# Strassen weight sums: from help in spare buffers to an adding transfer inside the raw buffer

## The chip, the cores and the metric

The kernel runs on one core of one Trainium2 chip. The metric is the device time of one execution in microseconds, as the median of the runs. A core has the engines TensorE (PE, with its weight loads shown apart as PEld), VectorE (DVE), ScalarE (ACT), GpSimd (POOL) and SyncE (SP), each of which works through its own queue in order, and 16 DMA engines that move data after SP, POOL or ACT has issued a transfer.

## The reference

One decoder block on x of 256 tokens by 4096 channels, all in float32:

```
h    = rmsnorm(x, norm_w)
proj = h @ w_in                     # 4096 x 20480: u_p z_p u_c b_c c_c z_c (2048 each), g_logit (8192)
y_pool = (pooled(u_p) @ pool_w) * pool_scale * silu(z_p)      # windows 2, 4, 8, 16, one per group of 512
y_conv = b_c * conv3(c_c * u_c) * silu(z_c)                   # causal, depthwise
br     = y_pool @ w_branch[0], y_conv @ w_branch[1]           # 2048 x 4096 each
merged = sum over both of sigmoid(g_logit + gate_b) * br
out    = rmsnorm(x + merged @ w_out, final_norm_w)            # 4096 x 4096
```

Nearly all of the arithmetic is in the products with `w_in`, `w_branch` and `w_out`: 256 rows against weights that are each used once.

## The kernel before

**Units and steps.** A unit produces 1024 output columns for all 256 tokens: `cu0`, `cc0`, `cz0`, `cb0` (the convolution branch), the same with 1, `pz`/`pu` (pooling), eight gate units `g0_0` to `g1_3`, eight branch units `b0_0` to `b1_3`, and four output units `o0` to `o3`. A unit of the input projection has 16 steps; each consumes one raw weight block of 256 x 1024, loaded as 128 partitions x 2048 floats (1024 KB) into one of `NRAW` raw buffers.

**Precision.** A float32 product is made of three fast ones: each operand is split into a high part (ACT copies it to the type fp32r) and a low part (DVE subtracts the high part from the original), and PE computes high x high, high x low, low x high. The split weights lie in a ring of `RING` KB per partition (class `Ring`, lines 211 to 238), from which a block is taken in preparation and returned as PE finishes with it.

**P and S steps.** A P step multiplies the block directly: 24 matmuls of 128 x 512. An S step uses a variant of Strassen's scheme on the 2 x 2 quarters q0, q1, q2, q3 of the block (128 x 512 each) and needs 21 matmuls, with seven weight operands: q1, q2, q3 as they are, and four sums. Before, these are V = (q0 + q1, q0 + q2), then W0 = V0 + q2 and W1 = W0 + q3. The other operands of the products, sums of quarters of the activations, are made once for each activation block (`sums_s`, lines 902 to 908). Of the 448 blocks of P and S steps, 216 belong to S steps. Which places in a unit are S steps is in the table `PLACES`.

**What an S step's preparation is** (`Step.micros`, lines 291 to 325): DVE makes V (`sums`), ACT copies q1 to q3 (`direct`), DVE makes W0, the low parts of q1 to q3 and W1, then ACT and DVE split V (`t13`) and W (`t24`). In some steps, the helped ones, V isn't made by DVE: q0 is loaded twice into a half of a finished result tile (E or R) while that stands empty, and a POOL transfer adds q1 and q2 to it on its way from HBM (`place_of_sum`, and lines 1269 to 1287 of `pump`). The table `HELPED` lists the candidates, and a candidate whose place isn't free in time isn't helped. 60 S steps are helped, 156 are not.

**What sets the order.** `tc.keep_in_program_order` fixes every engine's order to the order in which the program emits. `pump` (line 1257), called after each group of matmuls, emits loads (when the raw buffer that they go to has been released), adds, and the preparation of coming steps, up to `AHEAD` = 3 steps ahead of the step that PE multiplies and as far as the ring has room. Between these, `tick` emits one item of a queue of other work every six matmuls: joins of finished sums, activations, transposes, stores, fills. SP issues the weight loads, POOL the other transfers.

**The opening.** In the first unit, `cu0`, x is still being loaded. Steps 2 to 9 each also square a part of x for the first norm (`square`, line 1094): ACT squares 1024 columns (the first straight into `sq`, the others into V), and DVE adds V to `sq`. At step 10 PE sums `sq` over partitions, DVE makes the reciprocal root and two diagonal matrices, and at step 11 PE multiplies these out (`spread`, line 1114).

Of the kernel before, what the change touches and what calls it, by code (L numbers as in the profile page):

```python
# [26 lines left out]
F32 = mybir.dt.float32  # L27
# [18 lines left out]
RING = 62  # L46
NRAW = 3
# [9 lines left out]
def hybrid_block(ctx: ExitStack, tc: tile.TileContext, x, x_t, norm_t, w_first, w_in, pool_w, pool_scale,  # L57
# [8 lines left out]
    pin = tc.keep_in_program_order  # L66

# [21 lines left out]
    def move(dst, src):  # L89

        return pin(nc.gpsimd.dma_start(dst, src))
# [18 lines left out]
    V = sb("V", [P, 2, NH])  # L110
    W = sb("W", [P, 2, NH])
# [60 lines left out]
    warm = V[:, 0, 0:P].bitcast(BF16)  # L172
# [74 lines left out]
    def place_of_sum(i):  # L247

        return (E, R)[i // 2][:, i % 2].rearrange("p (i n) -> p i n", i=2)


    class Step:
# [7 lines left out]
        def micros(self):  # L260
# [30 lines left out]
            if self.kind == "S":  # L291
                q = r.rearrange("p (i n) -> p i n", i=4)

                helped = self.slot is not None
                v = place_of_sum(self.slot) if helped else V
# [22 lines left out]
                def t24(block):  # L318
                    self.b24 = block
                    t = piece(block, 0, 8).rearrange("p (i a n) -> p i a n", i=2, a=2)  # L320
                    self.h24, self.l24 = t[:, :, 0], t[:, :, 1]
                    act(self.h24, W)
                    sub(self.l24, W, self.h24.bitcast(F32))

                return self.pre + self.post + ([] if helped else [(0, None, sums)]) + [(12, lambda: not helped or self.added, direct), (8, None, t13), (8, None, t24)]
# [31 lines left out]
        def groups(self):  # L357
# [27 lines left out]
            elif self.kind == "S":  # L385
# [3 lines left out]
                         "N5": (Q5, self.h13, self.l13, 0, ("F", 0, 1)),  # L389
                         "N7": (Q7, self.h13, self.l13, 1, ("F", 1, 0)),  # L390
                         "N6": (Q6, self.h24, self.l24, 0, ("F", 1, 1)),
                         "N4": (A22, self.h24, self.l24, 1, ("E", 1, 1))}
                order = ("N3", "M2", "N4", "M1", "N5", "N7", "N6") if self.closing else (
                    "M1", "N3", "M2", "N5", "N7", "N6", "N4")
                v = self.op.block
                left = {}
                for nm in order:
                    o, h, l, i, bank = prods[nm]
                    mm = [(v(0, o), h[:, i]), (v(0, o), l[:, i]), (v(1, o), h[:, i])]
                    block = {"M": self.bd, "N": self.bd}[nm[0]] if nm in ("M1", "N3", "M2") else (  # L400
                        self.b13 if nm in ("N5", "N7") else self.b24)
# [77 lines left out]
    sums_from = [None, None]  # L479

    def e_done(n=2, which=0):

        def f():
            sums_from[which] = now[0] + n
        return f
# [57 lines left out]
    def put(dst, src):  # L543

        for k in range(2):
            move(dst[:, :, 1 - k], src.rearrange("p (q k) t -> p q k t", k=2)[:, :, k])
# [1090 lines left out]
```

## Time and profile before

| | |
|---|---|
| median of 3 runs | 2359.65 us (2359.35 to 2360.26) |
| profiled execution, first to last instruction (the span) | 2357.9 us |
| profiled execution's own time, span and what lies around it | no figure apart from the span is recorded; the median of the runs is 1.75 us above the span |
| PE, DVE, ACT, POOL busy | 2344.5, 2204.8, 1426.4, 125.0 us |
| moved by DMA | 597.89 MB, 254 GB/s on average |
| mean granted TensorE clock | 0.998 |

Rows of the profile read as follows. A row of the timeline has the start in us from the span's start, the length in us, the engine, the line of the kernel, the operation, what is written and read by the tiles' names, the size and how many instructions were merged (x2: two in a row); in brackets stands the idle time before it and what ended that. A row of waits says who waited for whom: us in total, times, the longest. Lines 69 and 72 are the helpers by which ACT's and DVE's operations are recorded, so operations are told apart by tiles and sizes: `ring<-raw` of 128x1536 on DVE are the low parts of q1 to q3 of an S step, `W<-W,raw` its second W.

### The profile page before, as it was taken

The numbers are of one execution on the slowest core, as the hardware profiler recorded it, in microseconds if no ns is written. First come the engines' busy times: TensorE is split into PE (matmuls) and PEld (weight loads), VectorE is DVE, ScalarE is ACT, GpSimd is POOL, SyncE is SP. The second block draws the span as 40 slices with busy tenths as digits, with TensorE's granted clock in tenths as the row PEclk, the third lists the DMA queues.
The fourth block names the chain that finished last, engine by engine and source line by source line (L and its number), as shares of the span: only waits on it lengthen the run. The fifth ranks groups of instructions, "written<-read, shape, count | busy, mean of one in ns | idle before, by whom it ended". The sixth has DMA issues, their size and how long they took to land.

```text
span 2357.9 us, 28175 instructions
## 1 busy us (share of the span) xinstructions
PE 2344.5 (99%) x10456; PEld 1941.8 (82%) x10456; DVE 2204.8 (94%) x2278; ACT 1426.4 (60%) x1485; POOL 125.0 (5%) x180
## 2 busy tenths in 40 slices
PE   9999999999999999999999999999999999999998
PEld 7888888888888888888888888888888888888886
DVE  8999999989999989989999999999999899898998
ACT  7555665656556556566565656665665556566564
POOL 0000000000002002000000000000000000000000
PEclk9999999999999999999999999999999999999999
DMA  8567787866877758757887887898866668777777
GB/s 336 182 229 228 238 272 256 272 231 215 269 262 250 234 218 258 230 220 248 263 267 259 286 270 243 259 302 289 292 237 233 246 244 306 225 244 274 253 235 269
DMA packets 110347, 597.89 MB, mean 254 GB/s; under 512 B 11504, under 2 KB 11760, under 8 KB 56704
## 3 DMA queue, kind: packets, MB, share of 16 engines
q1 hardware_dynamic: 89584, 508.37, 59.5%
q0 software_dynamic: 20192, 86.65, 15.7%
q8 instruction: 82, 1.34, 0.2%
q10 hardware_dynamic: 432, 1.07, 0.1%
q14 instruction: 57, 0.47, 0.1%
HBM read 563.20 MB, written 25.49 MB: 250 GB/s over the span
## 4 chain that ended last, share of the span: by engine, by line
PE 99%; DMA 0%; DVE 0%; ACT 0%; SPq 0%; DVEq 0%; issue 0%
PE sums L1336 72%; PE shared L1336 25%; PE shared L816 1%; PE shared L534 1%; DMA raw<-in_w_first_dram 0%; PE shared L795 0%; PE shared L796 0%; PE shared L798 0%; ACT V L69 0%; PE shared L797 0%; PE sums L1573 0%; DVE R L72 0%; DVE E L84 0%; DVE raw L1555 0%; ACT ring L69 0%; DVEq L1633 0%
## 5 line engine op out<-in xcount | busy, mean ns | idle before, releaser
L1336 PE MATMUL sums<-ring,arena 128*128 128x512 f32 x7497 | 1776.1, 390 | 0.7 <-ACT ring L69 0.7
L1336 PEld LDWEIGHTS sums<-ring,arena 128*128 128x128 f32 x7497 | 1404.7, 188 | 292.0 <-ACT ring L69 1.1
L72 DVE TENSOR_TENSOR ring<-raw,ring 128x1024 fp32r<-128x1024 f32 (+3 forms) x686 | 934.6, 1390 | 71.1 <-ACT ring L69 70.0
L69 ACT ACTIVATE ring<-raw 128x1024 fp32r<-128x1024 f32 (+3 forms) x686 | 792.2, 1189 | 210.6 <-PE sums L1336 133.9
L1336 PE MATMUL shared<-ring,arena 128*128 128x512 f32 x2556 | 645.0, 389 | 0.0
L1336 PEld LDWEIGHTS shared<-ring,arena 128*128 128x128 f32 x2556 | 479.5, 188 | 99.8 <-issue 0.3
L69 ACT ACTIVATE ring<-W 128x1024 fp32r<-128x1024 f32 x216 | 229.5, 1063 | 405.7 <-DVE W L72 352.7
L72 DVE TENSOR_TENSOR ring<-W,ring 128x1024 fp32r<-128x1024 f32 x216 | 264.7, 1225 | 17.4 <-ACT ring L69 5.1
L69 ACT ACTIVATE ring<-V 128x1024 fp32r<-128x1024 f32 x156 | 165.2, 1059 | 174.3 <-DVE V L72 152.8
L72 DVE TENSOR_TENSOR V<-raw 128x1024 f32<-128x1024 f32 x156 | 189.9, 1218 | 8.6 <-DMA raw<-in_w_in_dram 6.5
L72 DVE TENSOR_TENSOR ring<-V,ring 128x1024 fp32r<-128x1024 f32 x156 | 189.9, 1217 | 2.8 <-ACT ring L69 2.8
L72 DVE TENSOR_TENSOR W<-W,raw 128x512 f32<-128x512 f32 x216 | 148.1, 686 | 0.0
L72 DVE TENSOR_TENSOR W<-V,raw 128x512 f32<-128x512 f32 x156 | 107.8, 691 | 4.7
L72 DVE TENSOR_TENSOR R<-R,E 128x1024 f32<-128x1024 f32 (+1 forms) x49 | 77.4, 1591 | 3.9 <-ACT E L69 1.7
L72 DVE TENSOR_TENSOR R<-R,shared 128x512 f32<-128x512 f32 x87 | 59.5, 684 | 4.8 <-ACT R L69 3.0
L94 POOL DMA_DIRECT2D E<-in_w_in_dram x35 | 30.6, 875 | 599.3 <-DMA E<-in_w_in_dram 416.3
L69 ACT ACTIVATE arena<-sa 128x512 fp32r<-128x512 f32 (+2 forms) x50 | 26.2, 556 | 57.3 <-DVE sa L72 56.6
L69 ACT ACTIVATE E<-sums,rin 128x512 f32<-128x512 f32 x76 | 48.8, 681 | 11.0 <-PE sums L1336 11.0
L72 DVE TENSOR_TENSOR ring<-E,ring 128x1024 fp32r<-128x1024 f32 x44 | 54.0, 1226 | 1.5 <-ACT ring L69 1.5
L69 ACT ACTIVATE ring<-E 128x1024 fp32r<-128x1024 f32 x44 | 45.9, 1044 | 2.3 <-PE sums L1336 1.2
L72 DVE TENSOR_TENSOR ring<-R,ring 128x1024 fp32r<-128x1024 f32 (+1 forms) x22 | 29.1, 1323 | 4.0 <-ACT ring L69 4.0
L72 DVE TENSOR_TENSOR arena<-sa,arena 128x512 fp32r<-128x512 f32 (+2 forms) x50 | 28.5, 598 | 1.4 <-ACT arena L69 1.4
(149 smaller groups left out, 640.4 us busy)
## 6 DMA issues: line engine op xcount, KB each, us to landing
raw<-in_w_in_dram SPq DMA_DIRECT2D x265, 1024.0 KB, 5.1
raw<-in_w_branch_dram SPq DMA_DIRECT2D x64, 1024.0 KB, 5.1
raw<-in_w_out_dram SPq DMA_DIRECT2D x57, 1024.0 KB, 5.5
raw<-in_w_in_dram SPq DMA_DIRECT2D x53, 768.0 KB, 6.1
E<-in_w_in_dram SPq DMA_DIRECT2D x35, 512.0 KB, 7.3
E<-in_w_in_dram POOLq DMA_DIRECT2D x35, 512.0 KB, 8.9
R<-in_w_in_dram SPq DMA_DIRECT2D x18, 512.0 KB, 7.9
R<-in_w_in_dram POOLq DMA_DIRECT2D x18, 512.0 KB, 8.7
```

Source lines behind the costliest of these rows:

```text
L69: return pin(nc.scalar.activation(dst, src, func, **kw))
L72: return pin(nc.vector.tensor_tensor(out=dst, in0=a, in1=b, op=op))
L94: return pin(nc.gpsimd.dma_start(dst, src, accum_op=ALU.add))
L534: pin(nc.tensor.transpose(shared(j)[:, i * T + t * P:i * T + (t + 1) * P], src[:, t, c:c + P], ident))
L816: pin(nc.tensor.matmul(o, a[:, k, ts], b[:, k], start=(k, i) == (0, 0), stop=(k, i) == (3, 2)))
L1336: pin(nc.tensor.matmul(ps, lhs, rhs, start=n == 0, stop=n == u.total[b] - 1))
```

## The change

The first sum, q0 + q1, is made in the raw buffer itself: after the block has been loaded, a POOL transfer adds q1 to q0 within SBUF (128 x 512 floats, 256 KB). This holds for every S step; it is emitted when the load of the following block has been emitted. With q0 now standing for q0 + q1, DVE computes W = q0 - q2 into a tile of 512 columns, and after the low parts of q1 to q3 are made, subtracts W in place from q1 and q3 in one operation of 1024 columns. The four sums that PE needs are then q0 and W (`firsts`) and the new q1 and q3 (`seconds`); the sums of activations change their signs to match, and the products N6 and N7 change places in the order. The low parts of the sums are all made in `seconds`.

The places of sums in E and R, the broadcast loads, the adds from HBM, the table `HELPED` and what kept the account of free places are removed, and so is the tile V. The raw buffers become four instead of three. They are released when a step's preparation is whole; before, an S step's raw buffer was released as soon as `direct` had been emitted. `RING` goes from 62 to 60. The squares of the opening go through W, now 512 columns wide, in two halves; the last unit's squares go into a raw buffer that stands empty. In `pz1` and `g0_0`, which host the pooling steps, the P and S steps now stand in the order of the table `PLACES`, whose rows for these two change. Transfers of `move` get a queue as an argument, which is POOL's everywhere (`Q`).

```diff
-RING = 62
-NRAW = 3
+RING = 60
+NRAW = 4
+Q = "P" * 12
...
-    V = sb("V", [P, 2, NH])
-    W = sb("W", [P, 2, NH])
+    W = sb("W", [P, NH])
...
-                def sums(_):
-                    add(V, q[:, 0:1].to_broadcast([P, 2, NH]), q[:, 1:3])
-
                 def direct(block):
...
                     act(self.dh, q[:, 1:4])
-                    add(W[:, 0], v[:, 0], q[:, 2])
+                    sub(W, q[:, 0], q[:, 2])
                     sub(self.dl, q[:, 1:4], self.dh.bitcast(F32))
-                    add(W[:, 1], W[:, 0], q[:, 3])
-                    self.split = True
-
-                def t13(block):
...
+                def firsts(block):
...
+                    act(self.h02[:, 0], q[:, 0])
+                    act(self.h02[:, 1], W)
+                    sub(q[:, 1:4:2], q[:, 1:4:2], W[:, None].to_broadcast([P, 2, NH]))
+
+                def seconds(block):
...
-                    act(self.h13, v)
-                    sub(self.l13, v, self.h13.bitcast(F32))
-                    self.summed = True
...
+                    act(self.h13, q[:, 1:4:2])
+                    sub(self.l02[:, 0], q[:, 0], self.h02[:, 0].bitcast(F32))
+                    sub(self.l02[:, 1], W, self.h02[:, 1].bitcast(F32))
+                    sub(self.l13, q[:, 1:4:2], self.h13.bitcast(F32))
...
-                order = ("N3", "M2", "N4", "M1", "N5", "N7", "N6") if self.closing else (
-                    "M1", "N3", "M2", "N5", "N7", "N6", "N4")
+                order = ("N3", "M2", "N4", "M1", "N6", "N7", "N5") if self.closing else (
+                    "M1", "N3", "M2", "N5", "N6", "N7", "N4")
...
-        sub(q[:, Q5], a21, a22)
+        add(q[:, Q5], a21, a22)
         sub(q[:, Q6], q[:, Q5], a11)
-        sub(q[:, Q7], a11, a21)
-        add(q[:, Q3], a12, q[:, Q6])
+        sub(q[:, Q7], a21, a11)
+        sub(q[:, Q3], a12, q[:, Q6])
...
-            act(flat(V), src, AF.Square)
-            add(sq, sq, flat(V))
+            for n in range(2):
+                act(W, src[:, n * 2 * T:(n + 1) * 2 * T], AF.Square)
+                add(sq[:, n * 2 * T:(n + 1) * 2 * T], sq[:, n * 2 * T:(n + 1) * 2 * T], W)
...
-        elif s.slot is not None:
-            load(r[:, NH:], s.src.rearrange("p k n -> p (k n)")[:, NH:])
         else:
             load(r.rearrange("p (k n) -> p k n", k=2), s.src)
         s.raw = r
+        if s.kind == "S":
+            adding.append((state["nl"] + WAIT, s, r))
...
-    LEAD, WAIT = 4, 1
+    WAIT = 2
...
-            while adding and (adding[0][0] <= state["nl"] or adding[0][1].load_index < state["nl"]):
-                _, t, v, w = adding.popleft()
-                move_add(v.rearrange("p i n -> p (i n)"), w)
+            while adding and adding[0][0] <= state["nl"]:
+                _, t, r = adding.popleft()
+                move_add(r[:, 0:NH], r[:, NH:2 * NH])
                 t.added = True
```

How this moves instructions is shown at three places. The first is DVE in unit `cu1`, an unhelped S step and the P step behind it. Before,

```order
L72 TENSOR_TENSOR V<-raw 128x1024
L72 TENSOR_TENSOR W<-V,raw 128x512
L72 TENSOR_TENSOR ring<-raw,ring 128x3x512
L72 TENSOR_TENSOR W<-W,raw 128x512
L72 TENSOR_TENSOR ring<-V,ring 128x2x512
L72 TENSOR_TENSOR ring<-W,ring 128x2x512
L72 TENSOR_TENSOR ring<-raw,ring 128x1024 x2
```

and now:

```order
L74 TENSOR_TENSOR W<-raw 128x512
L74 TENSOR_TENSOR ring<-raw,ring 128x3x512
L74 TENSOR_TENSOR raw<-raw,W 128x2x512
L74 TENSOR_TENSOR ring<-raw,ring 128x512
L74 TENSOR_TENSOR ring<-W,ring 128x512
L74 TENSOR_TENSOR ring<-raw,ring 128x2x512
L74 TENSOR_TENSOR ring<-raw,ring 128x1024 x2
```

The 1024-wide V is gone, W stands once, the subtraction in place follows the low parts of the quarters at once, and one split of 1024 has become two of 512; the last row is the P step that follows.

The second place is POOL's queue in the gate units `g1_0` and `g0_1`, where results are stored (`gates_d`) and the gate's bias is added to R. Before, the adds from HBM into E and R stand between them:

```order
L91 DMA gates_d<-R 128x2048
L94 DMA R<-in_gate_b_dram 128x2x1024
L94 DMA E<-in_w_in_dram 128x1024
L91 DMA gates_d<-R 128x2048
L94 DMA E<-in_w_in_dram 128x1024
L94 DMA R<-in_w_in_dram 128x1024
L94 DMA R<-in_gate_b_dram 128x2x1024
```

and now:

```order
L93 DMA gates_d<-R 128x2048
L96 DMA raw<-raw 128x512 x5
L96 DMA R<-in_gate_b_dram 128x2x1024
L96 DMA raw<-raw 128x512 x2
L93 DMA gates_d<-R 128x2048
L96 DMA raw<-raw 128x512 x8
```

Seven to ten adds within SBUF now pass through POOL's queue in a unit, in line with its stores and bias adds. The third place is ACT in the opening unit `cu0`, around two of the squares, before:

```order
L69 ACTIVATE V<-E 128x1024
L69 ACTIVATE arena<-E,par_n 128x256 x2
L69 ACTIVATE ring<-raw 128x1024 x2
L69 ACTIVATE V<-E 128x1024
L69 ACTIVATE arena<-E,par_n 128x256 x2
```

and now:

```order
L71 ACTIVATE W<-E 128x512 x2
L71 ACTIVATE arena<-E,par_n 128x256 x2
L71 ACTIVATE ring<-raw 128x1024 x2
L71 ACTIVATE W<-E 128x512 x2
L71 ACTIVATE arena<-E,par_n 128x256 x2
```

Each square is now two operations that write the same 512 columns of W one after the other, with a sum on DVE reading W after each.

More of the change, by code (lines that the diff above doesn't have):

```diff
@@ L477, in halves @@
         return [lambda t=t: fn(t) for t in range(2)]
-    sums_from = [None, None]
     def e_done(n=2, which=0):
-        def f():
-            sums_from[which] = now[0] + n
-        return f
+        return None
     def combine(u):
@@ L848, in epi @@
                 return gap(2) + [lambda: mul(Y, R, Y)]
-            items = [lambda t=t: move(E[:, t], gates_d[n, c][:, t]) for t in range(2)] + gap(7)
+            items = [lambda t=t: move(E[:, t], gates_d[n, c][:, t], QUEUE[4]) for t in range(2)] + gap(7)
             def copy(j):
@@ L880, in epi @@
             return gap(1) + [
-                square] + halves(lambda t: mul(R[:, t], R[:, t], Y[:, 0])) + [lambda: move(o_d[c], R)]
+                square] + halves(lambda t: mul(R[:, t], R[:, t], Y[:, 0])) + [lambda: move(o_d[c], R, QUEUE[7])]
         def src(i):
@@ L1290, in pump @@
                 s = steps[i]
-                if s.src is None or s.raw is not None:
+                if s.src is None or s.raw is not None and (s.kind != "S" or s.added):
                     if state["micros"] is None:
@@ L1310, in hybrid_block @@
     for s in steps:
[L1311 to L1322 removed]
+        s.prepared = s.split = s.added = False
     def tick():
@@ L1427, in hybrid_block @@
             break
-        sums_from[:] = [None, None]
-        if u is units[1]:
-            e_done()()
-            e_done(2, 1)()
         for st in u.steps:
             assert st.prepared, (u.name, st.kind)
-            if st is u.steps[0]:
-                running[0] = u
-            if st is u.steps[-1]:
-                running[0] = None
-                assert all(t is None or t.summed for t in sums_in)
             run_step(u, st)
@@ L1496, in hybrid_block @@
                     f()
[L1497 removed]
+            move(E, xrows[:, :, 3 * NU:], QUEUE[11])
             join(last)
@@ L1508, in hybrid_block @@
         unpark(c)
+    spare = raw[:, (last_raw + 3) % NRAW, 0:NH]
     pre, pre_h, var_h, dev, mean = (sb(name, [P, 2]) for name in ("pre", "pre_h", "var_h", "dev", "mean_out"))
```

98 lines of the change are left out of this document (27 added, 71 removed), and 4 rows, old and new, of the table PLACES.

## The prediction

> **What bounds the kernel now.** First the page's first part and its chain of waits, then the waits of TensorE (PE) alone, then the busy times by stretch (length; busy us and instructions of PE, weight loads, DVE, ACT, POOL; granted clock; DMA share; GB/s).
>
> ```profile
> PE 2344.5 (99%) x10456; PEld 1941.8 (82%) x10456; DVE 2204.8 (94%) x2278; ACT 1426.4 (60%) x1485; POOL 125.0 (5%) x180
> PE 99%; DMA 0%; DVE 0%; ACT 0%; SPq 0%; DVEq 0%; issue 0%
> PE shared L1072 <- DVE rout L1077: 1.1, 1, 1.1
> PE sums L1336 <- ACT ring L69: 0.7, 1, 0.7
> 0.00:20.00 20.00, 18.19 (x79) 14.32 (x80) 11.79 (x20) 13.79 (x20) 0.85 (x7) 1.00 0.90 347
> 1200.00:1400.00 200.00, 200.00 (x883) 165.38 (x882) 192.90 (x182) 122.67 (x115) 13.21 (x15) 1.00 0.85 273
> 2340.00:2358.00 18.00, 6.28 (x34) 5.25 (x32) 9.41 (x24) 4.35 (x9) 0.00 (x0) 0.79 0.61 235
> ```
>
> PE is busy 200.00 of 200 us in the middle and idle only in the first 20 us (1.81) and the last 18 (11.72); its two listed waits come to 1.8 us. DVE at 94% is near its limit without being the bound. A busy PE could still hide stalls, so its pace matters. The next rows are PE in stage g0_1 (columns: start, length, instruction).
>
> ```profile
> 1236.95 0.84 PE L1336 MATMUL shared<-ring,arena 128*128 128x512 f32 x3
> 1238.99 2.20 PE L1336 MATMUL shared<-ring,arena 128*128 128x512 f32 x9
> 1241.71 0.84 PE L1336 MATMUL shared<-ring,arena 128*128 128x512 f32 x3
> ```
>
> One matmul takes 0.39 us (0.84 less two intervals), and nine end after 2.20, so they start (2.20 - 0.39)/8 = 0.226 us apart. An S step (21 matmuls) lasts 1241.71 - 1236.95 = 4.76 us, again 0.227 each; a P step (24) lasts 5.44. There is no slack inside this pace. The change leaves matmuls, their count and their shapes alone, so a gain can come only out of the idle ends, which it does not shorten. The question is whether the new preparation keeps ahead of PE as the old one does.
>
> **The change, part by part.** *DVE per S step.* From the same stage: a helped S step from 1232.55, an unhelped one from 1237.87, the next step from 1244.44.
>
> ```profile
> 1232.55 0.69 DVE L72 TENSOR_TENSOR W<-E,raw 128x512 f32<-128x512 f32 x1
> 1237.87 1.22 DVE L72 TENSOR_TENSOR V<-raw 128x1024 f32<-128x1024 f32 x1
> 1239.12 0.69 DVE L72 TENSOR_TENSOR W<-V,raw 128x512 f32<-128x512 f32 x1
> 1239.73 1.75 DVE L72 TENSOR_TENSOR ring<-raw,ring 128x1536 fp32r<-128x1536 f32 x1
> 1241.40 0.69 DVE L72 TENSOR_TENSOR W<-W,raw 128x512 f32<-128x512 f32 x1
> 1242.00 1.22 DVE L72 TENSOR_TENSOR ring<-V,ring 128x1024 fp32r<-128x1024 f32 x1
> 1244.44 2.35 DVE L72 TENSOR_TENSOR ring<-raw,ring 128x1024 fp32r<-128x1024 f32 x2
> ```
>
> Helped costs 5.32 us of DVE, unhelped 6.57. By starts, a 512-wide operation occupies DVE 0.60 us (1241.40 to 1242.00), the 1536-wide 1.67, a 1024-wide 1.14 (2.35 for two). The new step is 0.60 (W) + 1.67 + 0.12 for the in-place subtraction that must wait for the operation just ahead (as 1237.87 to 1239.12 is 1.25 and not 1.14) + 1.14 + 0.60 + 0.60 + 1.14 = 5.87. So 156 unhelped steps gain 0.70 each, 60 helped ones lose 0.55: 109 - 33 = 76 us less DVE work, all beside PE. Worth nothing in time; it adds lead.
>
> *ACT.* One 1024-wide copy becomes two 512-wide ones.
>
> ```profile
> L69 ACT ACTIVATE ring<-W 128x1024 fp32r<-128x1024 f32 x216 | 229.5, 1063 | 405.7 <-DVE W L72 352.7 <-PE sums L1336 42.9 <-PE shared L1336 10.1
> L69 ACT ACTIVATE ring<-raw 128x512 fp32r<-128x512 f32 x4 | 2.5, 632 | 2.3 <-DMA raw<-in_w_first_dram 2.3
> ```
>
> 216 x (2 x 0.632 - 1.063) = 43 us on an engine that is 60% busy: nothing.
>
> *The ring.* All blocks are multiples of 4 units; 62 units never held more of them than 60 do. Nothing.
>
> *The opening.* The squares of x went through V, 1024 wide; now W takes each half in turn, so ACT's second square waits for DVE's first sum, and that idles DVE.
>
> ```profile
> 30.07 1.22 DVE L72 TENSOR_TENSOR sa<-sa,V 128x1024 f32<-128x1024 f32 x1
> 34.26 1.22 DVE L72 TENSOR_TENSOR sa<-sa,V 128x1024 f32<-128x1024 f32 x1
> 59.21 1.23 DVE L72 TENSOR_TENSOR ring<-raw,ring 128x1024 fp32r<-128x1024 f32 x1 [1.50 <-ACT ring L69]
> 61.17 0.16 DVE L1085 TENSOR_SCALAR mean<-shared 128x2 f32<-128x2 f32 x1 [0.74 <-PE shared L1108]
> 62.67 0.28 DVE L1112 TENSOR_SCALAR std<-ident,rin 128x128 f32<-128x128 f32 x1
> 66.57 0.38 PE L1116 MATMUL shared<-diag,ones 128*128 128x128 f32 x2
> ```
>
> DVE's period was 34.26 - 30.07 = 4.19 us a step. The sum of 1.14 becomes 0.69 (first half to its end) + about 0.65 (square of the second, 0.632, with the hand-over) + 0.60 = 1.94, and ACT, held back, costs DVE another 0.2 to 0.4 before the next step: about 5.2, still under PE's 5.44. So DVE no longer pulls ahead in these seven steps and is 7 x 1.0 = 7 us later. What is late next is the norm: PE takes the diagonals at 66.57, DVE had them at 62.95 (3.62 spare), and DVE idled 1.50 + 0.74 = 2.24 before them. 7 - 5.86 = 1.1 us of stall, less what ACT's waits for PE in between (1.50 here, more before) give back: 0 to 2, I take 0.6. It falls once.
>
> *The load and the adding transfer.* This is the unknown: the S step's W now waits for load plus add. With four buffers it can begin when the step four earlier has been read. The shortest time from there to W is at a stage's start, where the S step comes third after two short P steps; here g0_1 on DVE, the first row being the step four earlier, the second the S step's first sum, the third its 1536-wide row:
>
> ```profile
> 1177.94 2.35 DVE L72 TENSOR_TENSOR ring<-raw,ring 128x1024 fp32r<-128x1024 f32 x2
> 1190.04 1.22 DVE L72 TENSOR_TENSOR V<-raw 128x1024 f32<-128x1024 f32 x1
> 1191.91 1.75 DVE L72 TENSOR_TENSOR ring<-raw,ring 128x1536 fp32r<-128x1536 f32 x1
> ```
>
> Free at 1180.29; W must start 0.60 ahead of 1191.91, at 1191.31: a window of 11.0 us. Deeper in a stage two or three of the three steps between are S steps: 2 x 5.87 + 2.28 = 14.0 or 17.6. What goes into it (issues, KB each, median us to landing; then POOL's time to issue):
>
> ```profile
> raw<-in_w_in_dram SPq DMA_DIRECT2D x265, 1024.0 KB, 5.1
> E<-in_w_in_dram POOLq DMA_DIRECT2D x35, 512.0 KB, 8.9
> R<-E POOLq DMA_DIRECT2D x4, 1024.0 KB, 8.4
> R<-E POOLq DMA_DIRECT2D x4, 512.0 KB, 7.3
> late_d<-sa POOLq DMA_DIRECT2D x1, 256.0 KB, 3.1
> L94 POOL DMA_DIRECT2D E<-in_w_in_dram x35: 848/860/1022, 112.4 to 1636.6; - x35
> ```
>
> A 256 KB add out of SBUF is in no row. Below: a plain 256 KB store, 3.1; above: the 512 KB adds out of HBM, 8.9. Nearest are the adds R<-E: 8.4 for 1024 KB, 7.3 for 512 KB issued in pairs; a half or quarter of these bytes gives me 6. With the load 5.1 and 0.1 for the hand-over the chain is 11.2 (8.3 to 14.1): 0.2 over the shortest window. Does that reach PE? The lead is thinnest at the S step whose 1536-wide row starts at 1239.73, ends at 1241.48 and is used at 1241.71: 0.23 us. Up to there the new DVE times give: third step, after W, 5.27 for 4.78 (-0.49); four unhelped steps, +2.8; the helped one, -0.55; the last one's V and W, 1.86 for 0.60 (+1.26): +3.0. So a chain of up to 11.0 + 0.2 + 3.0 = 14.2 is covered here and my 11.2 costs nothing. W that waits holds back, on DVE in order, the step's own 1536-wide row, the next steps' rows and the joins of finished sums; PE's banks wait for those.
>
> *Queues.* POOL gets 216 adds and loses 60 (180 instructions before); each sits in order behind stores, gate loads and bias adds, but is issued four or five steps ahead. Of HBM reads, 60 broadcasts and 60 adds of 0.5 MB each go and 60 loads grow by 0.25 MB: 45 MB less; the 216 adds move 54 MB inside SBUF instead, so the DMA share (0.85 in the middle stretch above) stays about there.
>
> Sum against the profiled execution: 2357.9 + 0.6 = 2358.5 of span; the median of the runs lies 1.75 above the span, so **2360.2 us**.
>
> **Rivals.** *The add lands late.* Place: the S step third in a stage, as in g0_1, in some ten stages. It decides from 14 us on. For it: the 8.9 of the adds that run beside loads gives 14.1, and at a stage's start the stores of gates and bias adds run too. Against: a quarter of 1024 KB. At 15.2 each such stage loses about 1 us, 10 in all, and the lost lead then spreads to denser places: 2368 to 2385.
>
> [...]
>
> *The opening stalls.* If each halved sum cost 1.4 us instead of 1.0, 2.8 us more reach the diagonals: 2363, still no change.
>
> *Faster.* Less DVE work and 45 MB less from HBM would have to raise PE's pace. PE's 0.227 us holds everywhere; the two waits give 1.8 us at most, 2358. A gain over 4.7 us has nowhere to come from.
>
> **How the numbers follow.** 0.2% of 2359.65 is 4.7 us, about what a measurement of this kernel tells from no change. My forecast with the opening's variants: 0.72 (2358.5 to 2364). Late add 0.20, POOL locked out 0.05, both slower, though a third of the latter stays within 4.7. Faster 0.03. So faster 0.03, same 0.73, slower 0.24. The range takes in the first part of the late add, 2358.5 to 2369, leaving out its tail.
>
> **What would show it.** Right: PE again 200.00 of 200 in the middle, PE waits of 1 to 3 us with one new near 66 us for the diagonals; DVE near 2160 us busy (by the rows' lengths an S step loses 156/216 x 1.22 for V, 0.69 for the second W and 1.22 for one low part, and gains 1.22 in place and 2 x 0.69: 216 x 0.19 = 41 us less); W waiting for raw<-raw in few steps, 0 to 2 us each; adds landing in 5 to 7 us. Wrong: PE idle for ACT or DVE on ring at the third to eleventh step of the gate stages, raw<-raw landing above 9 us, W's waits over 100 us in total, or POOL's issue far over 860 ns.

## The result, and the profile after

The changed kernel takes 2426.31 us (median of 4 runs, 2422.46 to 2428.63) against 2359.61 before: a ratio of 1.0281, with a 95% interval of 1.0266 to 1.0295. That is 67 us slower; 2360.2 was predicted, with a range to 2369. The profiled execution has a span of 2426.9 us, 69.0 more than before.

First the page: its busy times, its chain of waits, the group of the adds, and the issues of the loads and of the adds (KB each, median us to landing).

```profile
PE 2372.5 (98%) x10456; PEld 1945.3 (80%) x10456; DVE 2163.1 (89%) x2345; ACT 1444.8 (60%) x1708; POOL 253.4 (10%) x336
PE 60%; DVE 17%; DMA 13%; issue 7%; ACT 2%; POOL 0%; SPq 0%; DVEq 0%; POOLq 0%; ACTq 0%
L96 POOL DMA_DIRECT2D raw<-raw x216 | 188.6, 873 | 1921.1 <-DMA raw<-in_w_in_dram 731.6
raw<-in_w_in_dram SPq DMA_DIRECT2D x318, 1024.0 KB, 6.0
raw<-raw POOLq DMA_DIRECT2D x216, 256.0 KB, 6.3
```

PE was 99% of the chain; now 60%, and what took its place is DVE, transfers and the hand-overs between them. DVE's own work fell by 41.7 us, to 2163.1: 2160 was predicted. DVE isn't slower (a 512-wide W takes 0.686 us in the mean, as before), it waits. Its waits:

```profile
DVE ring L74 <- ACT ring L71: 69.9, 72, 4.8
DVE W L74 <- DMA raw<-raw: 65.0, 25, 11.1
DVE W L74 <- issue: 62.2, 14, 7.4
DVE Y L74 <- DMA Y<-gates_d: 8.2, 2, 4.4
```

W, the first operation of an S step that needs the add, waits 127.2 us in 39 places. The view gives no releaser for 14 of them ("issue"); by the trace each wait of W over 0.3 us ends within 0.5 us of the landing of the step's own add, so these are adds too. (Lines 71 and 74 of the changed kernel are the helpers of ACT and DVE.) Of PE's waits these are the longest:

```profile
PE shared L1287 <- DVE ring L74: 28.2, 17, 10.2
PE sums L1287 <- ACT E L71: 5.2, 4, 4.4
PE sums L1287 <- DVE ring L74: 4.1, 6, 1.0
```

All of PE's listed waits come to 43.1 us against 1.8 before, so 41.3 more, and PE's busy time rose by 28.0 with the same matmuls: 41.3 + 28.0 = 69.3, the whole difference but for rounding. Busy time hides two things here. PE starts a matmul every 0.227 us and each lasts 0.39, so one that starts up to 0.16 us late leaves no idle time. And the granted clock falls: by the trace it is at half in six stretches between 1157 and 2335 us, 30.7 us in all, where the kernel before has none but at its end. PE is busy for 22.9 of these, so about 11 of the 28.0 us are the clock's (an estimate: half of 22.9). The stretches that the prediction showed of before (length; PE, weight loads, DVE, ACT, POOL; granted clock; DMA share; GB/s) now read:

```profile
0.00:20.00 20.00, 18.88 (x79) 14.77 (x80) 11.77 (x20) 13.77 (x20) 0.84 (x7) 1.00 0.91 346
1200.00:1400.00 200.00, 197.32 (x861) 160.65 (x860) 184.35 (x185) 124.11 (x139) 24.63 (x28) 1.00 0.83 253
2409.00:2427.00 18.00, 6.64 (x35) 5.54 (x34) 10.14 (x29) 5.31 (x14) 0.00 (x0) 0.82 0.61 235
```

The ends are as they were. The middle is not: 861 matmuls in 200 us where there were 883, 22 x 0.227 = 5.0 us lost, of which only 2.68 show as idle.

**How a late add reaches PE.** The chain of waits in order of time (start, length, what) in stage g0_1, for the add of the W at 1253.15:

```profile
1237.74 8.41 DMA raw<-in_w_in_dram
1246.15 0.02 issue
1246.17 0.04 POOLq L96
1246.22 0.56 issue
1246.77 5.69 DMA raw<-raw
```

Load 8.41, hand-over to POOL 0.62, add 5.69: 14.7 us. This add landed 0.69 us before its W began, so that W still had no idle time ahead of it. The next two S steps, whose chains by the trace are 17.0 and 17.2 us, wait; on DVE and on PE (in brackets the idle time and what ended it):

```profile
1261.06 0.69 DVE L74 TENSOR_TENSOR W<-raw 128x512 f32<-128x512 f32 x1 [1.88 <-DMA raw<-raw]
1268.25 0.69 DVE L74 TENSOR_TENSOR W<-raw 128x512 f32<-128x512 f32 x1 [1.14 <-DMA raw<-raw]
1263.47 0.73 PE L1287 MATMUL shared<-ring,arena 128*128 128x512 f32 x2 [0.60 <-DVE ring L74]
1270.67 0.74 PE L1287 MATMUL shared<-ring,arena 128*128 128x512 f32 x2 [1.85 <-DVE ring L74]
```

Each of these two W's is followed 2.4 us later by a PE that waits for the low part made behind it. Not every late W reaches PE: at the place that the prediction had named, the third step of this stage (W at 1218.40), the chain was 13.45 us by the trace, W waited 3.06 us and PE not at all. The lead covered it there, and was gone at the 7th, 10th and 11th step.

**The longest stall** has another cause. POOL, then DVE, then PE in stage g1_0:

```profile
1143.16 0.86 POOL L96 DMA_DIRECT2D R<-in_gate_b_dram  x1 [4.06 <-DMA R<-E]
1151.08 0.86 POOL L96 DMA_DIRECT2D R<-in_gate_b_dram  x1 [7.05 <-DMA R<-E]
1151.67 1.16 POOL L96 DMA_DIRECT2D raw<-raw  x1
1161.60 0.69 DVE L74 TENSOR_TENSOR W<-raw 128x512 f32<-128x512 f32 x1 [11.13 <-DMA raw<-raw]
1164.01 1.22 PE L1287 MATMUL shared<-ring,arena 128*128 128x512 f32 x2 [10.19 <-DVE ring L74]
```

The add is issued with no idle time on POOL ahead of it: it stood behind a bias add that waited 7.05 us for an earlier transfer. By the trace its load had landed 13.2 us before.

### The profile page after: what moved, and what is told of

Its sections match the earlier page's. It is cut to its first block, busy times and chain, and to the rows that moved or that the text cites. A ratio compares the mean times of both kernels' runs of the same rounds, so it can differ in the third digit from the quotient of the medians.

```text
span 2426.9 us, 28741 instructions
## 1 busy us (share of the span) xinstructions
PE 2372.5 (98%) x10456; PEld 1945.3 (80%) x10456; DVE 2163.1 (89%) x2345; ACT 1444.8 (60%) x1708; POOL 253.4 (10%) x336
## 3 DMA queue, kind: packets, MB, share of 16 engines
q0 software_dynamic: 42656, 111.82, 21.6%
## 4 chain that ended last, share of the span: by engine, by line
PE 60%; DVE 17%; DMA 13%; issue 7%; ACT 2%; POOL 0%; SPq 0%; DVEq 0%; POOLq 0%; ACTq 0%
PE sums L1287 43%; PE shared L1287 14%; DVE ring L74 11%; DMA raw<-raw 8%; DMA raw<-in_w_in_dram 3%; DVE raw L74 2%; DVE W L74 2%; DVE R L74 1%; ACT ring L71 1%; PE shared L799 1%; DMA raw<-in_w_branch_dram 1%; PE shared L518 1%; DMA raw<-in_w_out_dram 1%; DVE sa L74 0%; DMA Y<-gates_d 0%
## 5 line engine op out<-in xcount | busy, mean ns | idle before, releaser
L71 ACT ACTIVATE ring<-raw 128x1024 fp32r<-128x1024 f32 (+2 forms) x1118 | 1115.1, 1053 | 717.6 <-DVE raw L74 447.3
L74 DVE TENSOR_TENSOR ring<-raw,ring 128x1024 fp32r<-128x1024 f32 (+2 forms) x1118 | 1337.8, 1222 | 65.8 <-ACT ring L71 64.4
L96 POOL DMA_DIRECT2D raw<-raw x216 | 188.6, 873 | 1921.1 <-DMA raw<-in_w_in_dram 731.6
L74 DVE TENSOR_TENSOR raw<-raw,W 128x1024 f32<-128x1024 f32 x216 | 264.6, 1225 | 7.0
L74 DVE TENSOR_TENSOR W<-raw 128x512 f32<-128x512 f32 x216 | 148.3, 686 | 128.2 <-DMA raw<-raw 65.0
L71 ACT ACTIVATE ring<-W 128x512 fp32r<-128x512 f32 x216 | 136.3, 631 | 107.0 <-DVE W L74 97.0
L74 DVE TENSOR_TENSOR ring<-W,ring 128x512 fp32r<-128x512 f32 x216 | 147.9, 685 | 0.0
L74 DVE TENSOR_TENSOR R<-R,E 128x1024 f32<-128x1024 f32 (+1 forms) x49 | 77.3, 1592 | 7.7 <-DMA R<-in_gate_b_dram 2.5
L74 DVE TENSOR_TENSOR R<-R,shared 128x512 f32<-128x512 f32 x87 | 59.6, 685 | 2.5
L74 DVE TENSOR_TENSOR arena<-sa,arena 128x512 fp32r<-128x512 f32 (+2 forms) x50 | 28.6, 599 | 1.4 <-ACT arena L71 1.4
L518 PE MATMUL shared<-ident,R 128*128 128x128 f32 x160 | 22.7, 272 | 0.9 <-DVE R L74 0.9
L74 DVE TENSOR_TENSOR Y<-R,Y 128x1024 f32<-128x1024 f32 (+1 forms) x8 | 14.0, 1755 | 10.6 <-DMA Y<-gates_d 8.2
L71 ACT ACTIVATE E<-sums 128x512 f32<-128x512 f32 x40 | 21.8, 589 | 2.6 <-PE sums L1287 2.3
L799 PE MATMUL shared<-ring 128*128 128x512 f32 x96 | 22.1, 389 | 0.0
L74 DVE TENSOR_TENSOR R<-R,Y 128x1024 f32<-128x1024 f32 (+1 forms) x16 | 21.5, 1355 | 0.3
```

Source lines behind the costliest of these rows:

```text
L71: return pin(nc.scalar.activation(dst, src, func, **kw))
L74: return pin(nc.vector.tensor_tensor(out=dst, in0=a, in1=b, op=op))
L96: return pin(nc.gpsimd.dma_start(dst, src, accum_op=ALU.add))
L518: pin(nc.tensor.transpose(shared(j)[:, i * T + t * P:i * T + (t + 1) * P], src[:, t, c:c + P], ident))
L799: pin(nc.tensor.matmul(o, a[:, k, ts], b[:, k], start=(k, i) == (0, 0), stop=(k, i) == (3, 2)))
```

## The experiments

The theory from these rows: the adds are late, and that is the whole loss. Its rivals: the rest of the change (the extra copy on ACT, the in-place subtraction, raw buffers held longer), the traffic itself, and POOL's queue. Diffs are against the changed kernel; ratios are to the kernel before, run beside it, with 95% intervals.

| kernel | us | ratio |
|---|---|---|
| no_add | 2361.40 | 1.0006 (0.9996 to 1.0015) |
| noadd56 | 2369.08 | 1.0039 (1.0024 to 1.0054) |
| traffic56 | 2384.22 | 1.0104 (1.0088 to 1.0119) |
| traffic_act | 2369.30 | 1.0039 (1.0024 to 1.0053) |
| after_act | 2413.72 | 1.0229 (1.0207 to 1.0252) |
| wait1 | 2461.15 | 1.0435 (1.0419 to 1.0451) |
| split_load | 2408.19 | 1.0207 (1.0187 to 1.0227) |
| dl_first | 2407.79 | 1.0201 (1.0185 to 1.0216) |
| copy | 2378.16 | 1.0082 (1.0065 to 1.0099) |
| quarter | 2375.37 | 1.0065 (1.0050 to 1.0080) |
| dve_add | 2429.27 | 1.0293 (1.0278 to 1.0308) |
| pool_add | 2469.79 | 1.0462 (1.0446 to 1.0477) |
| mixed_act | 2394.12 | 1.0151 (1.0134 to 1.0168) |
| combo2 | 2411.70 | 1.0218 (1.0203 to 1.0234) |
| sparse | 2369.60 | 1.0042 (1.0027 to 1.0057) |

### Without the adds

```diff
-                move_add(r[:, 0:NH], r[:, NH:2 * NH])
```

> The changed kernel without its 216 adding transfers: the sum q0 + q1 is left out, so every S step works with q0 alone; all else stays (four raw buffers, one W, in-place subtractions, halved copies). Late add (W waits for load, hand-over and add, and the add comes too late): the whole loss goes, 2360 to 2363 us, with PE idle only at the opening's diagonals (1 to 2 us) and at both ends. Rival, the rest of the change (the extra ACT copy, the in-place subtraction, raw buffers held until the whole step is prepared): most of the loss stays, 2410 to 2426 us.

2361.40 us. The loss goes, all but 1.5 us (from 0.9 less to 3.5 more than before, by the interval). PE's longest wait is now the one for the opening's diagonals; the next new one is 0.9 us.

```profile
PE 2345.1 (99%) x10456; PEld 1940.9 (82%) x10456; DVE 2166.3 (92%) x2345; ACT 1452.0 (62%) x1708; POOL 72.3 (3%) x120
PE shared L1093 <- DVE diag L1089: 1.6, 1, 1.6
raw<-in_w_in_dram SPq DMA_DIRECT2D x318, 1024.0 KB, 4.9
```

The rival of the rest of the change falls. The loads land in 4.9 us here and in 6.0 with the adds, so the traffic is still open.

### The adds' traffic without the wait

```diff
-RING = 60
+RING = 56
...
+    dummy = sb("dummy", [P, 2, NH])
...
-                move_add(r[:, 0:NH], r[:, NH:2 * NH])
+                move_add(dummy[:, t.load_index % 2], r[:, 2 * NH:3 * NH])
```

> The sum is left out as before, but 216 adding transfers of 256 KB still run at the same place in POOL's program, from the third quarter of the raw buffer into two spare buffers in turn that nobody reads; to make room the ring has 56 units instead of 60. So the transfers are there and W does not wait for them. Late add: 2360 to 2366 us. Rival, contention (54 MB more inside SBUF slow the weight loads, 6.0 us to landing against 5.1 before, and that is what starves the preparation): 2400 us or more, with W waiting for the loads.

2384.22 us, between the two expectations. So two more runs: the control with the smaller ring and no transfers, and the traffic with three sorts of transfer moved to ACT's queue.

```diff
-RING = 60
+RING = 56
...
-                move_add(r[:, 0:NH], r[:, NH:2 * NH])
```

> The kernel without the adds (sum left out), with the ring at 56 units instead of 60: the control for the kernel whose transfers go into spare buffers. If its 24 us came from the smaller ring: 2380 to 2385 us. If they came from the transfers themselves (POOL's queue, contention): 2361 to 2368 us, the ring being worth no more than the waits of 0.6 to 0.8 us that PE shows there at four places.

```diff
-Q = "P" * 12
+Q = "PAPPAAPPPPPP"
```

> The kernel whose 216 transfers go into spare buffers (sum left out, ring 56), with three other sorts of transfer moved from POOL's queue to ACT's: E<-z_d, E<-gates_d and Y<-gates_d. In that kernel DVE waits 14.2 us for Y<-gates_d and 7.2 for E<-z_d, which start right behind an add on POOL. Queue in order (an add that waits for its load holds up what stands behind it on POOL): these waits go and 12 to 16 us come back, 2366 to 2374 us. Contention inside the DMA engines: the same transfers stay late whatever queue they are in, 2380 to 2386 us.

The control takes 2369.08 us: the ring at 56 costs 7.7. The traffic adds 15.1 to that, and gives back 14.9 of it when the three sorts leave POOL's queue (2369.30). DVE's waits, of traffic56:

```profile
DVE Y L74 <- DMA Y<-gates_d: 14.2, 3, 5.7
DVE R L74 <- DMA E<-z_d: 7.2, 2, 3.9
```

and of traffic_act, where no wait for Y<-gates_d is left:

```profile
DVE R L74 <- DMA E<-z_d: 2.4, 2, 1.4
```

So 216 transfers of 256 KB cost nothing by what they move (2369.30 us against 2369.08), although the loads land later beside them (in 6.0 us, and in 4.9 in noadd56). They cost by where they stand: an add that waits for its load keeps back what stands behind it on POOL. Contention falls as a cost of its own; that the adds themselves land later beside loads is another matter, taken up below.

### POOL's queue in the changed kernel

The same line for `Q`, with the adds on the path.

> The changed kernel, all of it computed, with E<-z_d, E<-gates_d and Y<-gates_d on ACT's queue instead of POOL's. In the changed kernel DVE waits 8.2 us for Y<-gates_d, 2.3 for E<-z_d and 1.6 for E<-gates_d, 12.1 in all. If the queue in order on POOL is a cost of its own beside the late adds, most of that comes back: 2412 to 2420 us. If the late adds alone decide, and these waits only fill time that would be lost anyway: 2423 to 2429 us.

2413.72 us, 12.6 less than the changed kernel: as expected if the queue is a cost of its own. (The runs of the two kernels spread over 6 and 11 us; by the two intervals it is some 6 to 19.) The opposite dose makes the adds stand earlier on POOL:

```diff
-    WAIT = 2
+    WAIT = 1
```

> The changed kernel with each add written right behind its own load instead of behind the next one; on POOL's queue a good dozen of adds then come one place earlier, some of them ahead of a gate-bias add or a store that waits. If some of the loss comes from POOL's queue in order (at 1151.67 an add is issued 13.2 us after its load has landed, behind a bias add that waits 7.05 us, and PE then idles 10.19 us), that stall goes: 2412 to 2419 us. If all of it is load plus add against the window, nothing moves: 2423 to 2429 us.

2461.15 us: neither expectation. I had thought only of what an add stands behind, not of what stands behind an add. W waits about as long as in the changed kernel (122.4 us for 127.2), while the others, held up now by adds that wait on POOL for their loads, are late. DVE's waits, and behind them one of PE's:

```profile
DVE R L74 <- DMA E<-gates_d: 15.9, 4, 5.1
DVE R L74 <- DMA R<-in_gate_b_dram: 13.3, 1, 13.3
DVE R L74 <- DMA E<-z_d: 11.7, 2, 6.2
DVE Y L74 <- DMA Y<-gates_d: 7.4, 2, 4.2
PE shared L518 <- DVE R L74: 17.3, 5, 6.8
```

48.3 us for the four of DVE; in the changed kernel the same four come to 14.6 (1.6, 2.5, 2.3, 8.2). That the 34 us between them are about the 35 that the time grew is in part chance, since DVE's waits don't reach PE one for one. PE's side shows the path more directly: its wait for DVE's R is 17.3 us here and 0.9 in the changed kernel, all its listed waits grew by 18.2, and its busy time by 12.8.

### More room for the adds

An add that waits for half a load, and a W that comes one operation later:

```diff
+        elif s.kind == "S":
+            for k in range(2):
+                load(r[:, k * NU:(k + 1) * NU], s.src[:, k])
```

> Each S step's weights come in two loads of 512 KB, q0 and q1 first, so that the add waits for half a load. Late add: the add starts 1.5 to 2.5 us earlier. The profile lists 39 waits of W above 0.3 us, 127.8 us in all; 2.0 us off each leaves 60.1 and 2.5 us leaves 48.1, so PE's 67 us of loss fall to some 25 to 35: 2384 to 2396 us. Rival, the rest of the change: no gain, 2420 us or more. Should the add be slowed by the load it runs beside, it now also runs beside the second half of its own: then less is gained, 2400 to 2415 us.

```diff
-                    sub(W, q[:, 0], q[:, 2])
                     sub(self.dl, q[:, 1:4], self.dh.bitcast(F32))
+                    sub(W, q[:, 0], q[:, 2])
```

> Two lines exchanged: DVE makes the 1536-wide low part, which needs only the load, before W, which needs the add. This gives the adds 1.67 us more in every S step; nothing else is moved. Late add: each of the 39 waits of W shrinks by 1.67 us, 127.8 us to about 69, and of PE's 67 us of loss some 36 are left, and DVE now waits for ACT's high part at the head of a step, 0 to 10 us of PE's: 2396 to 2411 us. If the window did not decide, but POOL's queue or something in the step's own order: 2420 us or more.

Both gain 18 us: 2408.19, the case in which the add runs beside the second half of its own load (it lands in 6.6 us instead of 6.3, and W still waits 103.4 us), and 2407.79, within the range. There is a plainer reason for the small gain of the first: by the trace the half load that the add waits for lands in 5.3 us in the median, where the whole one took 6.0, so the add starts about 0.7 us earlier and not 1.5 to 2.5. Of dl_first DVE's waits show both sides of the exchange: W's fell by 70 us, a little more than expected, but the low part now waits for ACT's high part, 104.2 us for 69.9. Such a wait of DVE costs nothing where DVE is ahead (no_add has 132.8 us of it at 2361.40); here PE itself waits 6.2 us for ACT in two places, a row that the changed kernel's list doesn't have.

```profile
DVE ring L74 <- ACT ring L71: 104.2, 142, 5.4
DVE W L74 <- DMA raw<-raw: 57.1, 27, 9.0
```

### Why the adds take so long

Two stretches of the changed kernel, the issues in each with the median time to landing: from 876 to 881 us, where the load ahead has ended before the add's packets start, and from 1251.5 to 1261.5, where loads are in flight.

```profile
raw<-raw POOLq DMA_DIRECT2D x1, 256.0 KB, 3.2
...
raw<-in_w_in_dram SPq DMA_DIRECT2D x2, 1024.0 KB, 8.3
raw<-raw POOLq DMA_DIRECT2D x2, 256.0 KB, 8.8
```

3.2 us alone, 8.8 beside loads. The trace bears this out for the rest: the 18 adds with a load in flight for less than half of their time take 3.3 us in the median, the 69 with one in flight throughout 7.5 (3.9 to 11.9). Two runs ask what makes it so long there: the adding, or the size.

```diff
-                move_add(r[:, 0:NH], r[:, NH:2 * NH])
+                move(r[:, 0:NH], r[:, NH:2 * NH])
```

> The 216 adding transfers become plain copies of the same 256 KB (q1 onto q0), in the same place and with the same wait of W; the sum is left out. If adding (reading and writing the target) is what makes them slow: they land about 1.5 times sooner, 4 us in the median, and the time falls to 2385 to 2400 us. If they are slow because they share the DMA engines with the loads: nothing moves, 6 to 6.5 us in the median and 2418 to 2430 us.

```diff
-                move_add(r[:, 0:NH], r[:, NH:2 * NH])
+                move_add(r[0:32, 0:NH], r[0:32, NH:2 * NH])
```

> The adding transfers take 32 of the 128 partitions, 64 KB instead of 256 (three quarters of the sum are left out); place and waits are the same. In the changed kernel an add lands in 3.2 to 3.5 us when no other transfer is in flight and in 7 to 9 us beside a load. If its packets take turns with the load's in the same DMA engines, a quarter of them lands in 3 to 4.5 us also beside a load: the chain is then 6.0 + 0.6 + 4 = 10.6 us, within the 11.0 of the shortest window, the waits of W go, and what is left is POOL's queue in order (12.6 us by the run with three transfers on ACT's queue) and the opening: 2372 to 2382 us. If a transfer beside a load starts late whatever its size: 6 us and more in the median, 2400 us or more.

2378.16 and 2375.37 us. Each comes out as its first expectation has it, the copy's time lower still: the adding transfer is dearer than the copy of the same bytes, and a quarter of it costs what the copy costs. W's waits fall with it, from 127.2 us to 47.6 and 44.9. The pages' rows for POOL's queue (packets, MB, share of 16 engines' span) and for the transfers; of the changed kernel, of the one without adds, of copy, and of quarter:

```profile
q0 software_dynamic: 42656, 111.82, 21.6%
```

```profile
q0 software_dynamic: 11552, 55.19, 8.7%
```

```profile
q0 software_dynamic: 28832, 111.82, 15.0%
raw<-raw POOLq DMA_DIRECT2D x216, 256.0 KB, 4.0
```

```profile
raw<-raw POOLq DMA_DIRECT2D x216, 64.0 KB, 4.0
```

An add is (42656 - 11552) / 216 = 144 packets, a copy of the same 256 KB 80. Which of the two counts, the packets or the adding itself, these runs don't separate. A quarter of the size still takes 4.0 in the median: by the trace 2.4 with a load in flight for less than half of the time and 5.4 with one throughout, 3.0 us more, where the whole add has 4.2 more. So most of the delay beside a load doesn't go with size, and what makes it stays open. Plain is the slope: 2.3 us off the transfer's median, and 0.8 off the loads' (5.2 us in both), take 48 to 51 of the 67 us off the time. The changed kernel stands on the steep part of the curve.

### The sum on an engine

```diff
-                move_add(r[:, 0:NH], r[:, NH:2 * NH])
...
+                    add(q[:, 0], q[:, 0], q[:, 1])
                     sub(W, q[:, 0], q[:, 2])
```

> The sum q0 + q1 on DVE, 512 wide, at the head of each S step's work, no transfer (all is computed). It costs DVE 216 x 0.60 = 130 us more of issue, 149 of busy time: 2315 of 2360 us, 98%. If the adds' lateness is all that hurt, W waits for no transfer, and only DVE's density can cost: 2365 to 2400 us, with waits of PE for DVE in the densest stages. If DVE at 98% were still enough: 2361 to 2365.

2429.27 us, as slow as the transfer and above both expectations: DVE at 2308.0 us busy keeps PE waiting at many places, with no transfer for W to wait for. Its page's busy times and PE's longest wait:

```profile
PE 2376.3 (98%) x10456; PEld 1937.5 (80%) x10456; DVE 2308.0 (95%) x2561; ACT 1460.9 (60%) x1708; POOL 70.8 (3%) x120
PE shared L1287 <- DVE ring L74: 13.9, 18, 1.3
```

The same sum as an operation of POOL:

```diff
-                move_add(r[:, 0:NH], r[:, NH:2 * NH])
+                pin(nc.gpsimd.tensor_tensor(out=r[:, 0:NH], in0=r[:, 0:NH], in1=r[:, NH:2 * NH], op=ALU.add))
```

> The sum q0 + q1 as an addition on POOL itself, in the place of the transfer (all is computed). The chain is then load, hand-over and one POOL operation instead of a transfer of 3.2 to 14.9 us. Late add: with a POOL operation of up to some 3 us the chain is 5 + 0.6 + 3 = 8.6 us, within the shortest window of 11.0, and the waits of W go: 2362 to 2372 us, what is left being POOL's other transfers behind adds that wait for their loads. Rival (POOL and DVE get in each other's way, so that DVE's own rows lengthen or the POOL operation takes 5 us or more): 2390 us or more, with DVE's 1024-wide rows above the 1.22 us of before.

2469.79 us: the rival. Groups of operations (busy us, mean ns):

```profile
L1247 POOL TENSOR_TENSOR raw<-raw 128x512 f32<-128x512 f32 x216 | 378.6, 1753 | 1760.6 <-DMA raw<-in_w_in_dram 1166.3 <-DMA raw<-in_w_out_dram 236.4 <-DMA raw<-in_w_branch_dram 179.4
L74 DVE TENSOR_TENSOR ring<-raw,ring 128x1024 fp32r<-128x1024 f32 x678 | 863.4, 1314 | 44.6 <-ACT ring L71 43.8
L74 DVE TENSOR_TENSOR W<-raw 128x512 f32<-128x512 f32 x216 | 185.0, 857 | 0.0
```

The chain is short enough, and W has no wait in its row. But DVE's operations beside it lengthen: W from 0.686 to 0.857 us, the 1024-wide ones from 1.22 to 1.31, in all 202.6 us more of DVE's time (2365.7), which is more than the sum on DVE costs (144.9). These are means over two sorts: by the trace the 35 W's that begin while a POOL addition runs last 1.78 us in the median, the 8 that begin before the addition that they meet 0.68, and the 173 that meet none 0.68. So a W that begins second is held, by 1.1 us, and one that begins first is not; `R<-R,shared`, one of whose inputs is in PSUM, keeps its 0.69 us in the 18 cases where it begins while a POOL addition runs (0.683 us in the mean over all 87, 0.685 in the changed kernel). What holds it is not shown.

### Sums on DVE where the window is short

With the three sorts of transfer on ACT's queue, the sum goes to DVE in chosen S steps only: by a rule (95 steps), by the rule and with the low part first, and by the list of the 40 steps whose W had waited.

```diff
+            s.here = sum(t.kind == "S" for t in loaded[max(0, i - 3):i]) < 2
...
+                    if self.here:
+                        add(q[:, 0], q[:, 0], q[:, 1])
                     sub(W, q[:, 0], q[:, 2])
```

> All is computed. The three sorts of transfer on ACT's queue; and the sum on DVE (0.60 us more) in the 95 S steps that have at most one S step among the three loads before them, by transfer in the other 121. Of the 39 waits of W in the changed kernel 25 (88 of 127.8 us) are in the 95 steps. Late add: about 40 us of waits are left, some 20 us of PE's time, and DVE's 57 us more are bearable: 2372 to 2392 us. If the waits only moved on to the steps that keep the transfer: 2400 us or more.

> All is computed. All three together: the transfers on ACT's queue, the sum on DVE in those 95 steps, and the 1536-wide low part before W. Late add: the 40 us of waits left shrink by 1.67 us each (14 waits) to about 20, and PE loses some 10 us or less: 2362 to 2375 us. It can't come under the 2359.65 us of before, since PE there stands idle only at both ends. If DVE at the head of each step now waits for ACT's high part: 2375 to 2390 us.

```diff
+            s.here = s.host.steps.index(s) in HERE.get(s.host.name, ())
```

> All is computed. E<-z_d, E<-gates_d and Y<-gates_d on ACT's queue; the sum on DVE in those 40 S steps where W waited over 0.9 us for its add in the changed kernel or in the one with these three transfers on ACT's queue, by transfer in the other 176. If the late adds at these steps are what is left of the loss (2413.7 - 2359.8 = 54 us), W's 120 us of waits fall below 30, and DVE's 24 us more cost 0 to 8: 2363 to 2380 us. If the lateness moves on to the steps that keep the transfer: 2390 us or more. It can't come under the time of before, where PE idles only at the ends.

mixed_act takes 2394.12 us, just above its range. W's waits fell to 32.2 us, but two of 8.5 and 11.4 us are left at steps that keep the transfer, and by the trace 13.3 of the 14.1 us that PE waits there for DVE's ring (`PE shared L1293 <- DVE ring L74`) come 2.4 us behind three W's that waited for a late add. What the 57 us more of DVE's work cost is not shown. combo2 takes 2411.70, far above its first range: W waits 13.1 us only, but DVE waits 104.1 for ACT where mixed_act waits 74.8. That this is what makes it slower is argued, not shown: sparse has 103.4 us of the same wait. PE's waits for DVE's and ACT's ring rows are at 35 places instead of 10, and short. sparse takes 2369.60, within the range, and this is the one row left of W's waits for an add:

```profile
DVE W L75 <- DMA raw<-raw: 14.9, 8, 4.9
```

40 sums on DVE, 24 us of its time, bring back 44 us beside the 12.6 of the queue. So most of the lateness sat at those 40 steps and didn't move on; some 10 us above the kernel before are left. No version came under the kernel before, whose PE idles only at its ends.

## Why the prediction was wrong, point by point

- **PE is the bound and nothing can be gained:** right. No kernel here beat the one before.
- **DVE's work, the ring, ACT:** right in sign and effect. DVE 2163.1 (2160 predicted). ACT's rise was put at 43 us and is 25.6 in no_add (1452.0 - 1426.4), at no cost that no_add shows. The ring at 60 is harmless by no_add; at 56 it would have cost 7.7.
- **The opening:** 0 to 2 us with 0.6 taken; PE's wait for the diagonals is 1.5, and 1.6 in no_add.
- **The load and the adding transfer: this step failed.** Its sum was 5.1 + 0.1 + 6 = 11.2 us, at most 14.1, against a window of 11.0 and a cover of 14.2. The window and the cover at the place that it named were borne out: a chain of 13.45 us there, 3.06 us of W's wait, none of PE's. (One term of the cover is a little off: the third step after its W lasts 4.70 us by the rows' starts, 1191.91 to 1196.61, and not 4.78, which makes the cover 14.1.) The chain was mis-sized in each of its terms: the load is 6.0 in the median (loads run beside adds now), the hand-over 0.6, and the add's 6.3, so close to the 6 taken, is a median over cases of 3.2 and of 8.8. By the trace the adds of the steps that waited took 8.8 in the median, and their chains 15.7 (12.9 to 27.8), past the bound of 14.1 in 32 of 39. Nor does the chain alone decide: 35 of the other 177 chains were over 14.1 too, and their W's didn't wait. And the window was checked at one sort of place: "deeper in a stage 14.0 or 17.6" was set down as safe without setting the upper bound of the chain against it, and 14 of the 39 waits were at steps with two S steps among the three before.
- **POOL's queue at nothing: this step failed too.** "Issued four or five steps ahead" holds for the place in the program and not for the time: an add can't be issued before its load has landed, and until then POOL, in order, does nothing else (731.6 us of its idle time ahead of the adds end with a load, by the page's row). It cost 12.6 us by after_act, and the stall of 10.19 us the other way round, an add behind a bias add.
- **The rival "the add lands late"** was the case, with the right mechanism and with the signs named for it: W's waits over 100 us (127.2), PE idle for DVE at the third to eleventh step. Its price was too low: "about 1 us at ten stages" where 39 waits average 3.3 us, and a deciding point of 14 us where waits began with chains of 12.9. A chance of 0.20 and a top of 2385 came from treating the adds' spread as an error of the estimate. It was a spread between steps, and the dear adds sit where the loads follow one another closely: by the trace 29 of the 39 had another load in flight for the whole of their time, against 40 of the other 177.
- **The 0.05 for "POOL locked out":** no run shows DVE keeping POOL from issuing a transfer. An add's issue takes 0.857 us in the median and 1.46 at most, with DVE 89% busy. What the runs showed in its place is DVE held up by a computing POOL: in pool_add a W that begins while a POOL addition runs lasts 1.78 us instead of 0.68.

## What to carry to other kernels

When work goes from an engine to a transfer, set the transfer's slow cases (beside other transfers, 8.8 us here, not alone, 3.2, and not in the median, 6.3) against the shortest window at every sort of place, and count the load that it waits for as part of its chain. A queue in order is held up by what waits in it: ask both what the new instruction stands behind and what stands behind it, since moving it earlier made this kernel 35 us slower and taking its neighbours off the queue 12.6 faster. With PE at 200 of 200 us the only safe place for a wait is one whose lead has been measured; 40 well chosen sums on DVE were worth more than 216, 95 chosen by a rule, or none.

## What the hardware showed that was not expected

The longest stall of PE cost more than its length. Around these 10.19 us (columns as above, the clock after POOL):

```profile
1153.80:1164.00 10.20, 0.02 (x1) 0.00 (x0) 2.37 (x3) 1.26 (x2) 0.88 (x1) 0.68 0.74 178
1164.00:1168.00 4.00, 3.99 (x10) 3.17 (x11) 4.00 (x5) 2.67 (x3) 0.00 (x0) 0.54 0.00 0
1168.00:1178.00 10.00, 10.00 (x46) 8.24 (x45) 8.98 (x9) 7.25 (x8) 0.87 (x1) 1.00 0.79 256
```

For the 4 us after it the granted clock is 0.54, and PE, busy 3.99 us, does 10 matmuls where 4.00 / 0.227 = 17.6 would fit: some 1.7 us more lost, and entered as busy. The trace has the halving after shorter stalls too: after 3.19 us of idle time (0.53 from 1785.4 to 1789.0), 2.54 us (0.50 from 1522.7 to 1526.0) and 2.47 us (0.50 from 1498.8 to 1502.1), and none after the 1.85 us that end at 1270.67.

The adding transfer inside SBUF did not cost what its bytes cost as a copy: in the same place of the program 256 KB land in 6.3 us in the median as an add and in 4.0 as a copy (3.3 and 2.3 for those with a load in flight for less than half of their time).

In pool_add a DVE operation with both inputs in SBUF that begins while a POOL addition runs lasts about 1.1 us longer, at each of three widths: 1.78 us instead of 0.68 for the 512-wide W, 2.32 instead of 1.22 for a 1024-wide low part, 2.84 instead of 1.75 for the 1536-wide one (in the mean over all, 0.857, 1.314 and 1.790 us, against 0.686, 1.221 and 1.753 in the changed kernel).
